# Encoder layer on one core: the residual's gate computed beside the first attention units in four column tiles from 1 MB loads, with the interleaving constants set anew

## The chip, the cores and the metric

The kernel runs on one core of a Trainium2 chip. The metric is device microseconds (us) for one launch. A launch computes one layer for two independent requests of 1024 tokens each, one after the other; below they are called the first and the second group.

## The reference, cut to what matters

Per group, with D = 1024, x of 1024 x 1024 and a condition vector c of 1024:

```
mod = silu(c) @ w_ada + b_ada              # w_ada is 1024 x 3072
shift, scale, gate = split(mod, 3)
h = rms_norm(x) * (1 + scale) + shift
qa, ka, va, za, qb, kb, vb, zb, ga, gb = split(h @ w_in)
oa = gqa_attention(qa, ka, va) * silu(za)                  # 8 heads of 64
ob = headwise_norm(diff_attention(qb, kb, vb)) * silu(zb)  # 4 heads, two maps each
out = (sigmoid(ga) * (oa @ w_proj_a) + sigmoid(gb) * (ob @ w_proj_b)) @ w_out
y = x + gate * out
```

The case is about `gate`: the last third of w_ada (1024 x 1024, 4 MB), multiplied by silu(c) of both groups at once. It is needed only where y is formed, at the very end of a group. It is made once, during the first group, and both groups use it.

## The kernel before, in words

Everything is in f32. Most projections split each f32 operand into a rounded part and a rest (two fp32r tiles) and sum three products; others, among them the gate, are plain f32 matmuls, which the trace records as two passes each, a weight load and a matmul per pass. Wide operands lie in 1 MB buffers ("u", 15 of them); weights come through three 256 KB staging buffers ("st"), are split by ScalarE and GpSimd (L179, L181) and land in two weight buffers ("w"). All DMAs are issued on one queue, SP's.

One group goes through these stages. A head makes k, v and half of the q of branch A. Then the attention runs as a chain of units: phase 0 and phase 1 hold 16 units each of branch A, phases 2 to 5 hold 4 units each of branch B (one phase for each head). A unit's scores (L734, L735) go to PSUM, VectorE takes the maximum (L736), ScalarE the exponential (L738), VectorE transposes blocks (L771), four DMAs finish the transposition ("flip", L776, tile q), and the values' matmuls follow (L796, L797 for A, L836 for B). This chain is long and TensorE would idle beside it, so every phase is woven with projections. Three streams run together: the attention, the projection that the next phase needs (qa_gen, vb_gen, qkb_gen with L514), and "z units" (z_gen, L703: 24 matmuls of 512 columns, an eviction by L709, a store), which nothing needs until the end of the group. There are 48 z units in a group. Six of them go to the head, and Z_SHARE gives a number to each phase; the last phase takes what is left.

The function `weave` (L72) sets the order by hand: each stream has a declared length and a head start, and the stream that is least far along goes next. The constants Z_SHARE, Z_HEAD_A, ATT_W (a factor on the attention's length), IN_A and Z_A (head starts) set the pace of each phase. A scheduler then lays out each engine's instructions in one fixed order from this emission order and its own estimate of time.

The last phase (L1150) weaves the rest of the attention, a stream `gates` (gated_gen, L909: it loads attention outputs and z units back, multiplies them, splits them into u buffers; its last part is kept for later) and a stream `fill`. In the first group `fill` starts with the gate (gate_gen, L445), then the remaining z units, then the first 16 - TAIL of the 16 steps of branch A's merge (merge_gen, L953: 12 matmuls of 512 columns for a step, and a multiplication by VectorE, L987, with the sigmoid of a reloaded z unit). The other TAIL steps follow when the attention is over. During the attention, general PSUM work has three banks; after it (`alone[0] = True`), L121 lets it take two more. Branch B's merge and the output projection (out_gen, L990) end the group; L1010 reads the gate, `gatec`.

gate_gen before: for each half of the 1024 gate channels it takes one PSUM bank, and for each of 8 row chunks loads 256 KB through a staging buffer (L451) and issues one f32 matmul with 2 stationary columns, the two groups' silu(c), and 512 moving columns, all 8 summed in the bank (L452). VectorE copies the 2 x 512 result (L456), four small TensorE transposes turn it into columns (L459), and L461 adds the bias. The stream yields after every second chunk: 8 steps.

Of the kernel before, what the change touches and what calls it, by code (L numbers as in the profile page):

```python
# [12 lines left out]
F32 = mybir.dt.float32  # L13
F32R = mybir.dt.float32r
AF = mybir.ActivationFunctionType
ALU = mybir.AluOpType
AX = mybir.AxisListType
# [3 lines left out]
P = 128  # L21
T = 1024
D = 1024
NCH = D // P
# [10 lines left out]


Z_SHARE = (
    (7, 19, 5, 3, 3, 4),
    (9, 14, 7, 3, 2, 6),
)  # L40
Z_HEAD = (6, 6)
Z_HEAD_A = (-0.4, -0.45)
ATT_W = (
    (1.07, 0.837, 1.1, 0.95, 1.07, 1.52),
    (1.15, 1.354, 1.035, 1.15, 0.85, 1.069),
)
IN_A = (
    (0.1, 0.05, 0.2, 0.05, 0.15, 0.1),
    (0.1, -0.05, 0.45, 0.15, 0.15, 0.65),
)  # L50
Z_A = (
    (0.1, 0.0, 0.4, 0.0, 0.0, 0.0),
    (0.15, 0.05, 0.35, 0.15, -0.1, -0.1),
)
LAST_ATT, LAST_FILL = (44, 26)
GATED_A = -0.3
TAIL = 6
TAIL_A = 0.3
LAG = 2

SILU = 2

# [9 lines left out]
def weave(*streams):  # L72

    live = [[g, n, 0, ahead] for g, n, ahead in streams if n > 0]
    while live:
        s = min(live, key=lambda s: s[2] / s[1] - s[3])
        if next(s[0], None) is not None:
            s[2] += 1
        else:
            live.remove(s)  # L80
# [10 lines left out]
def kernel(ctx: ExitStack, tc: tile.TileContext, t: dict):  # L91
    nc = tc.nc
    ent = ctx.enter_context

    const = ent(tc.tile_pool(name="const", bufs=1))
    upool = ent(tc.tile_pool(name="upool", bufs=15))
    wpool = ent(tc.tile_pool(name="wpool", bufs=2))
    spool = ent(tc.tile_pool(name="spool", bufs=3))
# [12 lines left out]
    def nm(s):  # L111
        uid[0] += 1
        return f"{s}_{uid[0]}"

    def sbank():
        return ps_s.tile([P, 1024], F32, tag="s", name=nm("s"))
# [4 lines left out]
    def gbank():  # L121
        turn[0] += 1
        if alone[0] and turn[0] % 5 in (0, 2):
            return sbank()[:, :512]
        return fbank()

    def fbank():
        return ps_f.tile([P, 512], F32, tag="f", name=nm("f"))

    def utile():  # L130
        return upool.tile([P, 2048], F32R, tag="u", name=nm("u"))

    def chunks4(u):
        return u.rearrange("p (c n) -> p c n", c=4)
# [18 lines left out]
    def mtile(tag, shape, dt=F32, bufs=None):  # L153
        return mpool.tile(shape, dt, tag=tag, name=nm(tag), bufs=bufs)

    def rtile():
        return mtile("row", [P, 512], bufs=3)

    dma = nc.sync.dma_start
# [4 lines left out]
    w_ada = t["w_ada"][0]  # L164
# [3 lines left out]
    ident = const.tile([P, P], F32, name="ident")  # L168
# [2 lines left out]
    nc.vector.memset(ones_c, 1.0)  # L171
    nhalf = const.tile([P, 32], F32, name="nhalf")
    nc.vector.memset(nhalf, -0.5)


    def split_w(w, q, st):
# [11 lines left out]
    def load_w(pieces, early=False):  # L188

        w = wpool.tile([P, NCH, 2, 256], F32R, tag="w", name=nm("w"))  # L190
        sts = []
        for q in range(4):
            if early:
                if q % 2 == 0:
                    room = halves2(ptile())
                st = room[q % 2].rearrange("p (c n) -> p c n", c=2)
            else:
                st = spool.tile([P, 2, 256], F32, tag="st", name=nm("st"))
            sts.append(st)
            off = 0  # L200
            for src in pieces(q):
                n = src.shape[1]
                dma(st[:, :, off : off + n], src.rearrange("(c p) n -> p c n", p=P))
                off += n
            assert off == 256
            if not early:
                split_w(w, q, st)
        return (w, sts) if early else w

    def w_cols(mat, *cols):  # L210
        def pieces(q):
            return [mat[q * 256 : (q + 1) * 256, c : c + n] for c, n in cols]
        return pieces
# [16 lines left out]
    bcol = const.tile([P, 3, NCH], F32, name="bcol")  # L230
    gcol = const.tile([P, NCH], F32, name="gcol")
    cT = const.tile([P, NCH, 2], F32, name="cT")
    modc = const.tile([P, 2, NCH, 2], F32, name="modc")
    gatec = const.tile([P, NCH, 2], F32, name="gatec")
# [208 lines left out]


    def gate_gen():  # L445
        for half in range(2):
            acc = gbank()[:2]
            for k in range(NCH):
                st = spool.tile([P, 512], F32, tag="st", name=nm("st"))
                col = 2 * D + half * 512  # L450
                dma(st, w_ada[k * P : (k + 1) * P, col : col + 512])  # L451
                nc.tensor.matmul(acc, cT[:, k], st, start=(k == 0), stop=(k == NCH - 1))  # L452
                if k % 2:
                    yield 1
            row = rtile()[:2]
            nc.vector.tensor_copy(row, acc)  # L456
            ps = gbank()[:, :8].rearrange("p (c g) -> p c g", g=2)
            for c in range(4):
                nc.tensor.transpose(ps[:, c, :], row[:, c * P : (c + 1) * P], ident[:2, :2])  # L459
            cs = slice(half * 4, half * 4 + 4)  # L460
            nc.vector.tensor_tensor(  # L461
                out=gatec[:, cs], in0=ps, in1=bcol[:, 2, cs].unsqueeze(2).to_broadcast([P, 4, 2]), op=ALU.add
            )


    def ht_gen(g, ht):
# [105 lines left out]
    def pipelined(ht, w, front, back):  # L572
        pend = []
        for tt in range(NTT):
            ps = yield from proj_tt(ht, w, tt)
            pend.append((tt, front(tt, ps)))
            if len(pend) > LAG:
                back(*pend.pop(0))
# [20 lines left out]
    def v2(u):  # L599
        return u.rearrange("p (h n) -> p h n", h=2)  # L600
# [26 lines left out]
    def qa_gen(st, half):  # L627
        w = load_w(w_cols(w_in, (C_QA + half * 256, 256)))
        qs = [v2(utile()), v2(utile())]
        ht = st["ht"]  # L630
        st["qa"][half] = qs
        if half == 0:

            by_q(st["cosA"], st["sinA"], gqa, 16)

        def front(tt, ps):
            x3, s3 = rows(ps, 4, st["rsA"][:, half, tt])
            rope(x3, s3, st["cosA"][:, tt : tt + 1], st["sinA"][:, tt : tt + 1], 16, by_turns(tt))
            return x3

        def back(tt, x3):
            sl = slice(tt * P, (tt + 1) * P)
            pairs_T(x3, qs[0][:, :, sl], qs[1][:, :, sl])
            made[id(qs)] = tt + 1

        yield from pipelined(ht, w, front, back)
# [371 lines left out]
    def head(g, st, zs, late):  # L1018
# [3 lines left out]
        if g == 0:  # L1022

            for i in range(2):
                weave((islice(kva, 6), 6, 0.0), (islice(zs, 3), 3, 0.0))
                if i == 0:
                    late()
            weave((chain(kva, qa), 40, 0.0), (islice(zs, nz - 6), nz - 6, Z_HEAD_A[g]))
        else:
            weave((chain(kva, qa), 52, 0.0), (islice(zs, nz), nz, Z_HEAD_A[g]))  # L1030

# [48 lines left out]
    def until_next(att):  # L1080

        for mark in att:
            if mark is not None:
                return
            yield 1
# [16 lines left out]
    for g in range(2):  # L1102
        st = states[g]
        ht = st["ht"]
        load_tables_A(st)
        zs = chain(*[z_item(st, i) for i in range(12)])
        head(g, st, zs, late)
        alone[0] = False
        if g == 0:
            load_tables_B()  # L1110

        att = attention(units_of(st))

        def phase(k, *fs, more=()):
            n_att = 16 * (6 + PV_LAG) if k < 2 else 4 * (9 + PV_LAG)
            nz = 3 * Z_SHARE[g][k]
            weave(
                (until_next(att), n_att * ATT_W[g][k], 0.0), (chain(*fs), 31 * len(fs), IN_A[g][k]),
                (islice(zs, nz), nz, Z_A[g][k]), *more,
            )  # L1120

        phase(0, qa_gen(st, 1))
        phase(1, vb_gen(ht, st["vb"], 0), qkb_gen(ht, st["qkb"], 0))
        oT, mT = ([], []), ([], [])
        for h in range(4):
            fs = []
            if h < 3:
                fs.append(qkb_gen(ht, st["qkb"], h + 1))
            if h == 1:
                fs.append(vb_gen(ht, st["vb"], 1))  # L1130
            if h < 3:
                phase(2 + h, *fs)

        first = chain(*[gated_gen(st, i, hf, oT[hf]) for i in range(2) for hf in range(2)])
        then = [[gated_gen(st, i, hf, oT[hf]) for hf in range(2)] for i in (2, 3)]

        def gates():
            yield from first
            yield from chain(*then[0])

        def fill():
            if g == 0:
                yield from gate_gen()
            yield from zs
            drain(first)
            yield from islice(merge, 16 - TAIL)

        merge = merge_gen(st, 0, oT, mT)

        weave((until_next(att), LAST_ATT, 0.0), (fill(), LAST_FILL, 0.0), (gates(), 12, GATED_A))  # L1150
        alone[0] = True
        weave((merge, TAIL, 0.0), (then[1][0], 2, TAIL_A))
        weave((merge_gen(st, 1, oT, mT), 8, 0.0), (then[1][1], 4, 1.0))
        if g == 0:
            weave((out_gen(g, mT), 16, 0.0), (ht_gen(1, states[1]["ht"]), 13, -0.1))
        else:
            drain(out_gen(g, mT))
# [54 lines left out]
```

## Time and profile before

| | us |
|---|---|
| median of 3 runs | 1974.42 |
| lowest and highest run | 1972.81, 1974.46 |
| span of the profiled execution, first to last instruction | 1971.9 |
| TensorE matmuls busy (PE) | 1901.8 |
| TensorE weight loads busy (PEld) | 1619.1 |
| VectorE busy (DVE) | 1353.0 |
| ScalarE busy (ACT) | 1012.0 |
| GpSimd busy (POOL) | 680.9 |

The runs' times are for whole launches; the profiled execution shows its span, 1971.9 us, 2.5 us under the median of the runs. In the rows of the profile a name such as `f<-st,cT` means that the tile f (a PSUM bank) is written from st and cT. `x32` is a count of records; two numbers after a bar are busy time in us and the mean duration of one in ns. Matmul records overlap, because the next starts before the one before has drained: the pace is read from starts, not from durations. A number in square brackets on the timeline is the idle time of the engine before that piece, with what ended it.

### The profile page before, as it was taken

The numbers are of one execution on the slowest core, as the hardware profiler recorded it, in microseconds if no ns is written. First come the engines' busy times: TensorE is split into PE (matmuls) and PEld (weight loads), VectorE is DVE, ScalarE is ACT, GpSimd is POOL, SyncE is SP. The second block draws the span as 40 slices with busy tenths as digits, with TensorE's granted clock in tenths as the row PEclk, the third lists the DMA queues.
The fourth block names the chain that finished last, engine by engine and source line by source line (L and its number), as shares of the span: only waits on it lengthen the run. The fifth ranks groups of instructions, "written<-read, shape, count | busy, mean of one in ns | idle before, by whom it ended". The sixth has DMA issues, their size and how long they took to land. (4 is left out here: it accounts for less than half of the span.)

```text
span 1971.9 us, 30870 instructions
## 1 busy us (share of the span) xinstructions
PE 1901.8 (96%) x10466; PEld 1619.1 (82%) x10466; DVE 1353.0 (69%) x2165; ACT 1012.0 (51%) x1920; POOL 680.9 (35%) x958
## 2 busy tenths in 40 slices
PE   8999999999989999999999999999999999998999
PEld 3888888888878985778889788888888889776887
DVE  4658876786888577757465598768878766776641
ACT  4447655565655353464323576556666444447410
POOL 2363511442446251322235344114444426322210
PEclk9899999999999999999999999999999999999999
DMA  9125545556454345865641355555555334478431
GB/s 315 33 89 149 144 139 149 158 156 174 127 144 111 89 117 173 272 234 179 222 151 44 115 144 167 148 149 157 156 152 161 98 102 119 120 222 267 166 102 75
DMA packets 271614, 295.26 MB, mean 150 GB/s; under 512 B 37856, under 2 KB 220256, under 8 KB 271456
## 3 DMA queue, kind: packets, MB, share of 16 engines
q1 hardware_dynamic: 271456, 293.28, 50.1%
q8 instruction: 84, 1.38, 0.3%
q14 instruction: 74, 0.61, 0.1%
HBM read 133.72 MB, written 42.01 MB: 89 GB/s over the span
## 5 line engine op out<-in xcount | busy, mean ns | idle before, releaser
L703 PE MATMUL f<-u,w 128*128 128x512 f32 x2184 | 561.3, 395 | 3.0 <-ACT w L179 1.3
L514 PE MATMUL f<-w,u 128*128 128x256 f32 x3456 | 489.6, 286 | 5.2 <-ACT ev L709 2.7
L514 PEld LDWEIGHTS f<-w,u 128*128 128x128 f32 x3456 | 460.7, 192 | 26.8 <-ACT ev L709 3.7
L703 PEld LDWEIGHTS f<-u,w 128*128 128x128 f32 x2184 | 396.8, 189 | 78.1 <-ACT w L179 1.8
L181 POOL TENSOR_TENSOR w<-st,w 128x512 fp32r<-128x512 f32 x166 | 227.8, 1391 | 463.2 <-ACT w L179 412.9
L736 DVE TENSOR_REDUCE m<-s 128x1 f32<-128x1024 f32 x256 | 310.2, 1217 | 55.1 <-PE s L735 52.0
L771 DVE STREAM_TRANSPOSE p<-p 128x1024 f32<-128x1024 f32 x192 | 238.0, 1241 | 112.8 <-ACT p L738 110.2
L785 DVE TENSOR_TENSOR q<-q,hi 128x512 fp32r<-128x512 f32 x256 | 193.9, 774 | 47.9 <-ACT hi L784 46.4
L738 ACT ACTIVATE p<-s,m,rsB 128x1024 f32<-128x1024 f32 x128 | 154.0, 1204 | 135.0 <-DVE m L737 103.3
L738 ACT ACTIVATE p<-s,m,rsA 128x1024 f32<-128x1024 f32 x128 | 153.8, 1202 | 128.1 <-DMA q<-p 95.8
L735 PE MATMUL s<-u,sw 128*128 128x512 f32 x512 | 205.0, 401 | 0.0
L784 ACT ACTIVATE hi<-q 128x512 fp32r<-128x512 f32 x256 | 153.2, 624 | 78.2 <-DMA q<-p 50.2
L179 ACT ACTIVATE w<-st 128x512 fp32r<-128x512 f32 x196 | 114.2, 626 | 101.9 <-DMA st<-in_w_in_dram 46.6
L976 PE MATMUL f<-u,w 128*128 128x512 f32 x552 | 136.4, 400 | 11.3 <-ACT ev L709 4.1
L796 PE MATMUL a<-hi,u 128*128 128x256 f32 x512 | 132.0, 284 | 4.8 <-DVE oo L813 3.1
L976 PEld LDWEIGHTS f<-u,w 128*128 128x128 f32 x552 | 104.8, 192 | 35.3 <-DVE u L987 4.6
L836 PE MATMUL a<-q,u 128*128 128x256 f32 x512 | 125.9, 385 | 5.6 <-DMA q<-p 1.9
L797 PE MATMUL a<-q,u 128*128 128x256 f32 x512 | 129.8, 287 | 0.5 <-DVE q L785 0.4
L734 PE MATMUL s<-u 128*128 128x512 f32 x256 | 109.5, 428 | 7.9 <-ACT p L738 4.0
L734 PE MATMUL s<-u,u 128*128 128x512 f32 x256 | 103.3, 404 | 13.8 <-ACT p L738 9.0
L836 PEld LDWEIGHTS a<-q,u 128*128 128x128 f32 x512 | 95.9, 193 | 21.6 <-issue 2.9
L735 PEld LDWEIGHTS s<-u,sw 128*128 128x128 f32 x512 | 97.4, 190 | 15.5
(186 smaller groups left out, 2639.1 us busy)
## 6 DMA issues: line engine op xcount, KB each, us to landing
q<-p SPq DMA_DIRECT2D x768, 128.0 KB, 2.6
st<-in_w_in_dram SPq DMA_DIRECT2D x132, 256.0 KB, 3.0
zd<-ev SPq DMA_DIRECT2D x96, 256.0 KB, 2.2
sw<-u SPq DMA_DIRECT2D x256, 64.0 KB, 2.0
p<-zd SPq DMA_DIRECT2D x64, 256.0 KB, 3.8
u<-in_w_ada_dram SPq DMA_DIRECT2D x8, 1024.0 KB, 10.4
st<-in_w_in_dram SPq DMA_DIRECT2D x64, 128.0 KB, 2.7
st<-in_w_out_dram SPq DMA_DIRECT2D x32, 256.0 KB, 3.2
```

What stands on the lines that cost most here:

```text
L181: e.tensor_tensor(out=wl, in0=st, in1=wh.bitcast(F32), op=ALU.subtract)
L514: nc.tensor.matmul(ps, lt[c][:, sl], w[:, c, wi, :], start=(k == 0), stop=(k == 23))
L703: nc.tensor.matmul(ps, w[:, c, wi, e * P : (e + 1) * P], rt[c], start=(k == 0), stop=(k == 23),)
L734: nc.tensor.matmul(s[:, sl], q, k[:, sl], start=True, stop=False)
L735: nc.tensor.matmul(s[:, sl], sw, k[:, sl], start=False, stop=True)
L736: nc.vector.tensor_reduce(out=m, in_=s, axis=AX.X, op=ALU.max, negate=True)
L738: nc.scalar.activation(pt.rearrange("p (j c a) -> p j c a", j=4, c=8), s.rearrange("p (c a j) -> p j c a", c=8, j=4), AF.Exp, scale=rs, bi ...
L771: nc.vector.transpose(pt, pt)
L784: nc.scalar.activation(th, tl.bitcast(F32), AF.Copy)
L785: nc.vector.tensor_tensor(out=tl, in0=tl.bitcast(F32), in1=th.bitcast(F32), op=ALU.subtract)
L836: nc.tensor.matmul(acc, u["v"][:, k], pT[:, k], start=(k == 0), stop=(k == 7))
L976: nc.tensor.matmul(ps, w[:, c, wi, d * P : (d + 1) * P], o[:, oi, :], start=(k == 0), stop=(k == 11))
```

## The change

The gate leaves the last phase and becomes a fourth stream of the first group's phase 0, with declared length 12 and a head start of -0.2. It comes in four pieces n, one for each half of the channels and each half of the rows. A piece is one load of 1 MB into a u buffer; then a PSUM bank is zeroed by VectorE and four f32 matmuls (2 stationary columns, 512 moving columns) write to partitions 0, 32, 64 and 96 of the bank, each with its own column tile of the TensorE array and each started and stopped by itself, so that nothing is summed in the bank; ScalarE copies the bank to SBUF. Four more f32 matmuls with the copied rows as 128 x 128 stationary operand and a constant 128 x 2 matrix `two` as the moving one both transpose and sum the four partial rows. VectorE adds the bias for the first half of the rows, and the earlier result for the second.

The last phase's fill loses the gate, gets one more z unit in the first group (taken from phase 1), and TAIL falls from 6 to 3 in both groups, so three more merge steps are emitted in the last phase. The other constants of the weaving change too, in both groups.

```diff
 Z_SHARE = (
-    (7, 19, 5, 3, 3, 4),
+    (7, 18, 5, 3, 3, 5),
     (9, 14, 7, 3, 2, 6),
 )
-Z_HEAD_A = (-0.4, -0.45)
+Z_HEAD_A = (-0.4, -0.5)
 ATT_W = (
     (1.07, 0.837, 1.1, 0.95, 1.07, 1.52),
-    (1.15, 1.354, 1.035, 1.15, 0.85, 1.069),
+    (1.133, 1.218, 1.035, 1.15, 0.917, 1.069),
 )
 IN_A = (
-    (0.1, 0.05, 0.2, 0.05, 0.15, 0.1),
-    (0.1, -0.05, 0.45, 0.15, 0.15, 0.65),
+    (0.15, 0.05, 0.2, 0.05, 0.25, 0.1),
+    (-0.1, -0.15, 0.45, 0.25, 0.15, 0.85),
 )
 Z_A = (
-    (0.1, 0.0, 0.4, 0.0, 0.0, 0.0),
-    (0.15, 0.05, 0.35, 0.15, -0.1, -0.1),
+    (0.1, 0.0, 0.2, 0.05, 0.0, 0.0),
+    (0.15, 0.05, 0.45, 0.15, -0.1, -0.1),
 )
-LAST_ATT, LAST_FILL = (44, 26)
+LAST_ATT = (45, 44)
+LAST_FILL = (24, 26)
-TAIL = 6
+TAIL = 3
+GATE_A = -0.2
...
+    two = const.tile([P, 2], F32, name="two")
+    nc.vector.tensor_reduce(
+        out=two, in_=ident.rearrange("p (j r) -> p r j", j=4)[:, :2, :], axis=AX.X, op=ALU.add
+    )
...
     def gate_gen():
-        for half in range(2):
-            acc = gbank()[:2]
-            for k in range(NCH):
-                st = spool.tile([P, 512], F32, tag="st", name=nm("st"))
-                col = 2 * D + half * 512
-                dma(st, w_ada[k * P : (k + 1) * P, col : col + 512])
-                nc.tensor.matmul(acc, cT[:, k], st, start=(k == 0), stop=(k == NCH - 1))
-                if k % 2:
-                    yield 1
-            row = rtile()[:2]
-            nc.vector.tensor_copy(row, acc)
+        for n in range(4):
+            half, q = n // 2, n % 2
+            wt = chunks4(utile().bitcast(F32))
+            row, col = q * 512, 2 * D + half * 512
+            dma(wt, w_ada[row : row + 512, col : col + 512].rearrange("(c p) n -> p c n", p=P))
+            yield 1
+            acc = gbank()
+            nc.vector.memset(acc, 0.0)
+            for c in range(4):
+                nc.tensor.matmul(
+                    acc[32 * c : 32 * c + 2], cT[:, q * 4 + c], wt[:, c], start=True, stop=True,
+                    tile_position=(0, 32 * c),
+                )
+            part = rtile()
+            nc.scalar.activation(part, acc, AF.Copy)
+            yield 1
             ps = gbank()[:, :8].rearrange("p (c g) -> p c g", g=2)
             for c in range(4):
-                nc.tensor.transpose(ps[:, c, :], row[:, c * P : (c + 1) * P], ident[:2, :2])
-            cs = slice(half * 4, half * 4 + 4)
-            nc.vector.tensor_tensor(
-                out=gatec[:, cs], in0=ps, in1=bcol[:, 2, cs].unsqueeze(2).to_broadcast([P, 4, 2]), op=ALU.add
-            )
+                nc.tensor.matmul(ps[:, c, :], part[:, c * P : (c + 1) * P], two, start=True, stop=True)
+            g = gatec[:, half * 4 : half * 4 + 4]
+            b = g if q else bcol[:, 2, half * 4 : half * 4 + 4].unsqueeze(2).to_broadcast([P, 4, 2])
+            nc.vector.tensor_tensor(out=g, in0=ps, in1=b, op=ALU.add)
+            yield 1
...
-        phase(0, qa_gen(st, 1))
+        phase(0, qa_gen(st, 1), more=((gate_gen(), 12, GATE_A),) if g == 0 else ())
...
         def fill():
-            if g == 0:
-                yield from gate_gen()
             yield from zs
...
-        weave((until_next(att), LAST_ATT, 0.0), (fill(), LAST_FILL, 0.0), (gates(), 12, GATED_A))
+        weave((until_next(att), LAST_ATT[g], 0.0), (fill(), LAST_FILL[g], 0.0), (gates(), 12, GATED_A))
```

## The prediction, made before the run

> **What bounds the kernel now.** I read the page's first and second part, then stretches of the span, then the timeline where the gate runs.
>
> ```profile
> span 1971.9 us, 30870 instructions
> PE 1901.8 (96%) x10466; PEld 1619.1 (82%) x10466; DVE 1353.0 (69%) x2165; ACT 1012.0 (51%) x1920; POOL 680.9 (35%) x958
> PE   8999999999989999999999999999999999998999
> ```
>
> TensorE (PE) is busy in 1901.8 of 1971.9 us, in every stretch but the first and a few later ones; the next engine, VectorE, stands at 69%. So the time is TensorE's work at its pace, plus 70 us of idle. A change can do three things: alter what TensorE has to issue, remove or add idle, or put work where there was idle. The idle is spread; here are stretches of the first group's last phase, of the same places in the second group (whose last phase has no gate), and of the phases that receive the gate. Columns: stretch, its length, PE busy (records), granted clock, share of the DMA engines, GB/s.
>
> ```profile
> 751.00:790.00 39.00, 35.18 (x125) 1.00 0.68 206
> 821.00:850.00 29.00, 24.89 (x109) 0.94 0.94 305
> ...
> 1711.00:1750.00 39.00, 39.00 (x179) 1.00 0.60 177
> ...
> 1781.00:1810.00 29.00, 22.36 (x97) 0.94 0.84 282
> ...
> 140.00:350.00 210.00, 203.32 (x1198) 0.99 0.53 146
> 350.00:560.00 210.00, 204.41 (x1189) 1.00 0.56 155
> ...
> 1100.00:1310.00 210.00, 202.33 (x1162) 0.99 0.53 146
> 1310.00:1520.00 210.00, 203.22 (x1208) 0.99 0.56 154
> ```
>
> The gate runs at 751 to 790 and there PE idles 39.00 - 35.18 = 3.8 us; at the same place of the second group it idles for nothing. After the attention's last scores it is the other way round: 4.1 us in the first group (821 to 850), 6.6 in the second (1781 to 1810). Phases 0 and 1 idle 6.7 and 5.6 us of 210 each: they have little room for more work.
>
> **The change, part by part.**
>
> *The gate's matmuls.* Old price first, from the lines grouped by shape (busy us, mean ns, idle before) and from PE's timeline.
>
> ```profile
> L452 PE MATMUL f<-st,cT 128*2 128x512 f32 x32 | 15.2, 592 | 1.5 <-DMA st<-in_w_ada_dram 1.5
> L459 PE MATMUL f<-ident,row 2*128 2x2 f32 x8 | 0.8, 202 | 0.8 <-DVE row L456 0.8
> ```
>
> ```profile
> 751.14 2.74 PE L452 MATMUL f<-st,cT 128*2 128x512 f32 x6
> ...
> 754.38 0.50 PE L858 MATMUL f<-ones_c,at 128*128 128x1 f32 x4
> 754.74 0.49 PE L734 MATMUL s<-u 128*128 128x512 f32 x1
> ...
> 767.73 0.40 PE L459 MATMUL f<-ident,row 2*128 2x2 f32 x4 [0.77 <-DVE row L456]
> 768.07 1.02 PE L452 MATMUL f<-st,cT 128*2 128x512 f32 x2
> ```
>
> Sixteen f32 matmuls are 32 passes. Six passes last 2.74 us from first start to last end and one lasts 0.592, so they start (2.74 - 0.592) / 5 = 0.43 us apart: 32 x 0.43 = 13.8 us. Four transposes take 768.07 - 767.73 = 0.34 us, eight 0.7. Removed: 14.5 us.
>
> Added: four groups of four matmuls, each again two passes of 0.43 us, now on four column tiles. No row here has column tiles, so I bound it. If a tile's pass starts only when the pass before has gone through, a group is 8 x 0.43 + the last pass's tail of 0.592 - 0.43 = 0.16, 3.6 us; if all four tiles stream at once, 2 x 0.43 + 0.16 = 1.0 us. I take a value between. The rows show the passes one behind the other in program order, and the two passes of one matmul need the same tile with other weights, so the second must follow the first. Then in a fixed order only the second pass of one tile and the first of the next can run together: 5 slots, 5 x 0.43 + 0.16 = 2.3 us for a group, 9.2 us for four.
>
> The Trainium skill bears on that from both sides. "TensorE: Matmul & The Clock Gate", Part 3, says that matmuls start and end in strict program order, which is what my five slots use, but it also measured three column tiles at 2.38 times the speed of one, for single passes. By that factor alone, 13.8 us would become an estimated 5.8. "TensorEngine Tiling (Array Packing)", Key Properties, speaks against the change: a change of tiling mode drains the engine, and there would be two in each group. With the tail above as the drain, the second would add 4 x 0.16 = 0.6 us. No run of this case yet shows either.
>
> Then 16 f32 matmuls with a full 128 x 128 stationary operand and 2 columns. The nearest row is L858 (one column): four passes from 754.38 to the next start at 754.74, 0.09 us each. It is lowest there because a load was already made; at the start of the kernel eight such passes stand in a row:
>
> ```profile
> 53.69 1.63 PE L273 MATMUL f<-ones_c,q 128*128 128x1 f32 x7
> 55.18 2.91 PE L703 MATMUL s<-u,w 128*128 128x512 f32 x6
> ```
>
> One of the eight records is missing from the trace; 55.18 - 53.69 = 1.49 us over eight is 0.19 each. Thirty-two passes are then 2.9 to 6.1 us; as the new ones come eight in a row, I take 0.155 us, between the two, 5.0 us. Sum of this edit: -14.5 + 9.2 + 5.0 = **-0.3 us**, with ends 4 x 1.0 + 2.9 - 14.5 = -7.6 and 4 x 3.6 + 6.1 - 14.5 = +6.0.
>
> *The waits around the old gate.* The 3.8 us of idle at 751 to 790 go with it: 1.5 is L452 waiting for its loads and 0.8 is L459 for VectorE, by the rows above; the rest fits the bank that the gate holds from its first matmul to L456, leaving two of three. What takes its place as cover is 24 matmuls of the extra z unit and 36 of three merge steps. Their pace:
>
> ```profile
> 789.73 8.45 PE L703 MATMUL f<-u,w 128*128 128x512 f32 x36
> ```
>
> (8.45 - 0.39) / 35 = 0.23 us, so 60 make 13.8 us, about the 14.5 that leave: the attention keeps its cover. I take **-3.8**; the ends are -3.8 and 0, since the second group, without a gate, loses as much a little later.
>
> *TAIL from 6 to 3.* Three merge steps for each group come into the regime of three banks. The early steps do wait there:
>
> ```profile
> 1784.80 5.78 PE L976 MATMUL f<-u,w 128*128 128x512 f32 x24 [2.61 <-DVE u L987]
> ...
> 1799.12 3.03 PE L976 MATMUL f<-u,w 128*128 128x512 f32 x12 [0.99 <-DVE u L987]
> ...
> 1819.59 8.46 PE L976 MATMUL f<-u,w 128*128 128x512 f32 x36
> ```
>
> But steps 11 to 13, the ones that move, are the last row: 36 matmuls, back to back, in f banks already, with the attention over. I take **0**, with 6 x 0.99 = 6 us as the upper end.
>
> *Phase 0 with the gate, phase 1 without one z unit.* Of the 15 u buffers phase 0 holds 14 (8 for the normalised input, 2 for k and v, 4 for q), so the four 1 MB loads go through one buffer, and each waits on SP's queue for the matmuls of the one before; behind it wait the flips (L776), the q swaps (L593) and the next weights (L203). The stream's three steps per piece stand a twelfth of the phase apart, about 210 / 12 = 17 us:
>
> ```profile
> L250 SPq DMA_DIRECT2D u<-in_w_ada_dram x8: 368/485/2545, 1.2 to 20.7; - x8
> ...
> DMA to landing us min/median/max: 5.4/10.4/12.6
> ```
>
> ```profile
> L776 SPq DMA_DIRECT2D q<-p x133: 542/602/1927, 147.9 to 347.9; - x133
> ...
> DMA to landing us min/median/max: 2.5/2.6/4.0
> ```
>
> A load takes 10.4 us to land, under 17, so the gate itself should find its data. What a flip (2.6 us) loses beside it is the third rival below; here 0. In issues SP gains: 16 become 4.
>
> The zeroing of the bank is a new wait: four matmuls stand behind a VectorE instruction, and all of TensorE behind them.
>
> ```profile
> L736 DVE TENSOR_REDUCE m<-s 128x1 f32<-128x1024 f32 x256 | 310.2, 1217 | 55.1 <-PE s L735 52.0
> 200.00:350.00 150.00, 144.58 (x862) 127.22 (x861) 109.39 (x156) 85.01 (x164) 42.30 (x39) 1.00 0.53 147
> ```
>
> It costs nothing when the order gives it time, and 4 x 1.2 = 4.9 us if each stands behind one reduction. The nearest row is L459's, 0.8 for two: I take **+0.8**. The engines' own time is free: VectorE is busy 109 and ScalarE 85 of 150 us there, and four zeroings, four copies and four additions are under 2 us for each piece.
>
> Against that stands cover. The two phases together get 14.2 us of gate and lose one z unit of 24 x 0.23 = 5.5: 8.7 us more independent work beside the same attention, whose waits there are (PE's waits in 130 to 350, then in 350 to 560; total, times, longest):
>
> ```profile
> PE s L734 <- DMA q<-p: 2.2, 2, 1.4
> PE s L734 <- ACT p L738: 1.4, 2, 0.8
> ...
> PE s L734 <- DMA q<-p: 3.9, 2, 3.6
> PE s L734 <- ACT p L738: 0.8, 1, 0.8
> ```
>
> That is 8.3 us. The order is fixed, so new work shortens a wait only where it happens to stand before it: 0 to -8.3, and I take a quarter, **-2.0**.
>
> *The constants.* They move work within a phase and remove none. The second group, where most of them change, idles 7.7 + 6.8 us in its two long stretches against 6.7 + 5.6 in the first group; bringing one to the other is worth 2.2. I take **0**, with 2.2 either way. The constant `two` is made in the first microseconds, before TensorE has any data, and costs nothing.
>
> **Sum:** -0.3 - 3.8 + 0 + 0.8 - 2.0 = -5.3 us, 1971.9 - 5.3 = 1966.6 of span. The median of the runs lies 2.5 us above the profiled span; with that kept, **1969.1 us**, 0.27% below 1974.42. What a measurement of this kernel can tell from no change is about 0.2%, 3.9 us, so faster means below 1970.5.
>
> **The rivals.**
>
> 1. *All four tiles stream at once.* A group is 1.0 us and not 2.3: 5.2 us less, 1963.9. For it: the tiles share no output partitions, and the compiler may order passes so that no tile waits. Against: passes stand in pairs in every f32 row here. The Trainium skill's section on packing, named above, starts tiles about 4 ns apart.
> 2. *Column tiles bring nothing.* A group is 3.6 us: 4 x 1.3 = 5.2 us more, 1974.3, no change. This is the change not doing what it says; no row speaks for tiles yet.
> 3. *Slower: the 1 MB loads hold up the flips.* A flip's packets share the 16 engines with a load that takes 10.4 us, and the scores behind it wait. The longest wait for a flip in these phases is 3.6 us; if each load makes one, 4 x 3.6 = 14.4 us, 1983.5. It decides from (5.3 + 3.9) / 4 = 2.3 us for each load on. For it: those 3.6 us exist with 256 KB weights as the largest neighbours. Against: the DMA engines are at 0.53 there, and cover stands in the weave.
> 4. *Merge steps wait for banks,* 6 us: 1975.1, no change.
>
> **How the numbers follow.** Forecast 0.38 (its own range 1965 to 1973, three quarters of it under 1970.5), rival 1 0.24, rival 2 0.15, rival 3 0.18, rival 4 0.05. Faster: 0.29 + 0.24 = 0.53. Within 0.2%: 0.09 from the forecast, 0.12 from rival 2, 0.04 from rival 4, 0.25. Slower: 0.18 + 0.03 + 0.01 = 0.22. The range reaches down past rival 1 with some of the cover's lower end, to 1960, and up into rival 3's milder half, to 1980.
>
> **What would show it.** Starts of the tiled passes: a group's eight records within 1.0 us (rival 1), 2.2 (forecast) or 3.5 (rival 2). The records on `two` at 0.09 to 0.19 us apart. No idle where the last phase's gate stood, as in the second group. The landing time of L776's flips in phase 0: near 2.6 us (forecast) or well above, with more waits of L734 on q<-p (rival 3). L976's waits on L987 in both groups no larger. The forecast is wrong if phase 0 gains more idle than the last phase loses, or if the new constants move more than 2.2 us.

## The result and the profile after

The changed kernel takes 1974.12 us (median of 20 runs, 1965.49 to 1991.98) against 1974.44 us for the kernel before (20 runs, 1969.18 to 1979.46). The ratio is 1.0000 with a 95% interval of 0.9987 to 1.0014: no change that can be measured. The forecast of 1969.1 us was 5 us too low, though inside its range; the case that came out had been given 0.25. That the time lies inside the range is luck, as the account step by step below shows: two large errors nearly cancelled.

The first lines of the page of the changed kernel:

```profile
span 1972.5 us, 30913 instructions
PE 1895.7 (96%) x10490; PEld 1625.9 (82%) x10490; DVE 1361.4 (69%) x2170; ACT 1017.6 (52%) x1928; POOL 674.0 (34%) x958
```

TensorE is busy for 6.1 us less, and the span is 0.6 us longer, so idle grew by 6.7 us, from 70.1 to 76.8. First, is the new gate as cheap as it should be? Its two lines in the changed kernel (L462 the tiled matmuls, L471 those on `two`), grouped by shape, then pieces of it on PE's timeline:

```profile
L462 PE MATMUL f<-u,cT 128*2 128x512 f32 x32 | 6.0, 702 | 0.2 <-DVE f L460 0.2
L471 PE MATMUL f<-two,row 128*128 128x2 f32 x32 | 4.5, 264 | 0.0
```

```profile
205.23 1.04 PE L462 MATMUL f<-u,cT 128*2 128x512 f32 x8
206.20 0.44 PE L579 MATMUL f<-ident,row 128*128 128x128 f32 x2
...
216.93 0.95 PE L471 MATMUL f<-two,row 128*128 128x2 f32 x8
217.74 0.36 PE L808 MATMUL a<-hi,u 128*128 128x256 f32 x1
...
238.96 1.03 PE L462 MATMUL f<-u,cT 128*2 128x512 f32 x6
239.92 0.50 PE L746 MATMUL s<-u,u 128*128 128x512 f32 x1
...
241.05 1.02 PE L462 MATMUL f<-u,cT 128*2 128x512 f32 x2
242.00 0.74 PE L526 MATMUL f<-w,u 128*128 128x256 f32 x4
...
269.19 1.89 PE L462 MATMUL f<-u,cT 128*2 128x512 f32 x8
271.01 0.58 PE L808 MATMUL a<-hi,u 128*128 128x256 f32 x1
```

Nearly. The eight passes of the first piece take 206.20 - 205.23 = 0.97 us: all four tiles stream at once, as in rival 1. The eight passes on `two` take 0.81 us, 0.10 each. The second piece was laid out in two parts, six passes and two, with scores between them, and each part takes as long as a whole piece (0.96 and 0.95 us). The last pair of lines shows something else: eight passes took 1.82 us at 269.19, because TensorE ran at half its clock there (a granted clock of 0.50 from 265.55 to 272.38). Read from the starts in this way, with half-clock time counted half, the new gate's work is 4.8 + 3.2 = 8.1 us. The old gate's, whose 32 passes were laid out in eight runs, is 15.7 us in the same reading; the prediction's count had 14.5.

Now the stretches that the prediction showed for before, in the changed kernel (same columns), with the first group's stretch of 690 to 751 as well, which stands first for the kernel before:

```profile
690.00:751.00 61.00, 60.76 (x357) 1.00 0.40 110
```

```profile
690.00:751.00 61.00, 58.26 (x350) 1.00 0.42 109
751.00:790.00 39.00, 39.00 (x181) 1.00 0.53 146
790.00:821.00 31.00, 30.53 (x136) 1.00 0.78 226
821.00:850.00 29.00, 21.98 (x91) 0.88 0.93 279
```

The idle at the old gate's place is gone, as forecast (39.00 of 39.00), but 2.7 us stand just before it and 7.0 us after it, where before had 0.2 and 4.1. To compare whole stages, here they are by their own landmarks: first scores, first values of branch B, first output matmul, the second group's first scores and first output matmul. First before, then the changed kernel:

```profile
140.70:561.10 420.40, 408.83 (x2388) 0.99 0.54 151
561.10:932.70 371.60, 359.88 (x1872) 0.99 0.54 164
932.70:1096.00 163.30, 162.83 (x913) 1.00 0.40 135
1096.00:1881.00 785.00, 756.83 (x4227) 0.99 0.53 152
```

```profile
142.70:567.00 424.30, 411.72 (x2408) 0.98 0.59 155
567.00:931.30 364.30, 352.62 (x1878) 0.99 0.56 160
931.30:1100.60 169.30, 166.07 (x920) 0.99 0.40 133
1100.60:1881.50 780.90, 753.28 (x4223) 0.99 0.56 153
```

Phases 0 and 1 grow by 3.9 us, the rest of the first group's attention and its merge shrink by 7.3, the output and the second group's head grow by 6.0, the second group's attention shrinks by 4.1; the start is 2.0 longer. So from its first scores to its first output matmul the first group did become 3.4 us shorter. The start, ahead of the first scores, has the same matmuls in both kernels in almost the same order, and it took between 137.1 and 142.9 us in the profiles of all the kernels below; its 2.0 us, with 3.4 us of added idle in them, need not be the change's.

**Half-clock time.** The granted clock is not a blur. In the trace it is either 1.00 or 0.50, and the halves come in pieces of 3.41 us or multiples. These are the stretches at half clock in the two kernels, up to the last microsecond, cut to the first and the last and the sum (columns as above), first before, then after:

```profile
43.21:46.62 3.41, 3.41 (x18) 0.50 0.48 57
...
1794.25:1797.66 3.41, 3.41 (x11) 0.50 0.63 216
sum 40.97, PE 39.93; mean PE 4.44
```

```profile
43.68:47.10 3.42, 3.42 (x19) 0.50 0.69 71
...
265.55:272.38 6.83, 6.83 (x32) 0.50 0.45 106
...
1777.65:1787.89 10.24, 5.86 (x14) 0.50 0.72 228
sum 58.04, PE 52.26; mean PE 4.02
```

What brings them on is seen best where the changed kernel stalls for 4.9 us (four stretches of 3.41 us, then PE's waits there):

```profile
1217.88:1221.29 3.41, 2.30 (x16) 1.00 0.23 45
1221.29:1224.70 3.41, 0.00 (x0) 1.00 0.79 192
1224.70:1228.11 3.41, 3.02 (x13) 0.50 0.51 132
1228.11:1231.53 3.42, 3.42 (x18) 1.00 0.68 215
```

```profile
PE a L808 <- DVE oo L825: 4.9, 1, 4.9
```

Here an idle window of 3.41 us is followed by one at half clock. I cut both profiles into windows of this length, starting where the trace changes the clock, and took those after the first 60 us. All 16 in which PE was busy for less than 1.5 us were followed by half clock, and so were all 141 such windows in the fourteen profiles below. Of the 10 with 1.6 to 2.1 us, three were. Of those with more that ran at full clock, none was. Two things stay unexplained: three windows that were at half clock themselves, with PE busy for 2.45, 2.78 and 3.41 us, were followed by another at half clock; and in the first 60 us half clock also followed windows that were wholly busy (39.79 to 43.21 and 46.62 to 50.03 in the kernel before). So a stall that leaves less than 1.5 us of a window busy costs itself and then up to 1.7 us for each half-clock window behind it, which is one window in most of these cases and two or three in some. The Trainium skill, "TensorE: Matmul & The Clock Gate", Part 1, describes this gate: two states, a free-running window of about 3.4 us, half rate after an idle window. The trace agrees in the states and the length; here windows that were up to 1.49 us busy already counted as idle.

With that the span can be split in three: idle (span less PE's busy time), the half-clock loss (half of PE's busy time in half-clock stretches), and the rest, TensorE's work as it would be at full clock. All kernels of this study, in us of the profiled execution, with the ratio of the runs to those of before:

| kernel | span | idle | half-clock loss | rest | ratio, 95% interval |
|---|---|---|---|---|---|
| before | 1971.9 | 70.1 | 20.0 | 1881.8 | |
| changed | 1972.5 | 76.8 | 26.1 | 1869.6 | 1.0000 (0.9987 to 1.0014) |
| before_no_gate | 1977.9 | 86.6 | 27.5 | 1863.8 | 1.0052 (1.0036 to 1.0068) |
| after_no_gate | 1976.4 | 85.7 | 27.4 | 1863.3 | 1.0053 (1.0034 to 1.0073) |
| before_tiles_last | 1996.7 | 91.4 | 33.0 | 1872.3 | 1.0153 (1.0132 to 1.0173) |
| after_one_tile | 1972.1 | 72.7 | 18.4 | 1881.0 | 1.0036 (1.0017 to 1.0056) |
| before_tiles_phase0 | 2010.0 | 98.7 | 41.0 | 1870.3 | 1.0157 (1.0137 to 1.0177) |
| after_old_second | 1988.0 | 86.2 | 29.2 | 1872.6 | 1.0068 (1.0050 to 1.0087) |
| after_nudge | 1982.3 | 83.7 | 26.6 | 1872.0 | 1.0037 (1.0021 to 1.0053) |
| before_nudge | 1986.8 | 79.8 | 25.9 | 1881.1 | 1.0068 (1.0051 to 1.0086) |
| before_nudge_down | 1970.9 | 67.7 | 21.6 | 1881.6 | 0.9995 (0.9978 to 1.0012) |
| after_nudge_z | 1987.3 | 84.8 | 27.9 | 1874.6 | 1.0032 (1.0017 to 1.0047) |
| before_no_gate_nudge | 1991.1 | 92.7 | 34.8 | 1863.6 | 1.0097 (1.0070 to 1.0124) |
| after_no_gate_nudge | 1980.2 | 86.6 | 29.0 | 1864.6 | 1.0016 (1.0000 to 1.0031) |

The rest sorts the kernels by their gate: the three with the old gate have 1881.1 to 1881.8, the six with tiles 1869.6 to 1874.6 (mean 1871.9), the four without a gate 1863.3 to 1864.6 (mean 1863.8), and the new gate with one tile in place of four has 1881.0. By that the old gate's work is worth 17.7 us and the new one's 8.1, and the change takes 12.2 us out of TensorE's work between the two profiles. Idle (+6.7) and half-clock time (+6.1) bring it back.

Not all of the 12.2 is the gate's: 4.5 us of it lie in the start, the output and the second group, whose matmuls the change does not touch, and no run shows why. The first group alone, from its first scores to its first output matmul, is sharper: a rest of 762.2 to 762.5 us with the old gate, 754.0 to 756.0 with tiles, 745.8 to 747.3 without a gate and 764.5 with one tile. There the old gate is worth 15.9 us and the new one 8.4, which agrees with their starts (15.7 and 8.1), and the change takes out 7.7. A profile is one execution, and some lie off the median of their kernel (before_tiles_phase0 was 8 us above it, after_nudge_z 9 above, after_one_tile 7 below); the first group's rest stays within 2 us for kernels of one gate all the same.

### The profile page after: what moved, and what is told of

It reads as the page before. It is cut to its first block, busy times and chain, and to the rows that moved or that the text cites. A ratio compares the mean times of both kernels' runs of the same rounds, so it can differ in the third digit from the quotient of the medians.

```text
span 1972.5 us, 30913 instructions
## 1 busy us (share of the span) xinstructions
PE 1895.7 (96%) x10490; PEld 1625.9 (82%) x10490; DVE 1361.4 (69%) x2170; ACT 1017.6 (52%) x1928; POOL 674.0 (34%) x958
## 4 chain that ended last, share of the span: by engine, by line
PE 60%; DVE 12%; DMA 10%; issue 5%; SPq 5%; ACT 4%; POOL 2%; ACTq 0%; POOLq 0%; DVEq 0%
PE f L715 14%; PE f L526 14%; DMA q<-p 5%; PE f L1017 5%; PE f L988 4%; PE a L848 4%; PE s L1017 4%; SPq L788 4%; PE s L746 4%; PE s L747 3%; DVE m L748 3%; DVE q L797 3%; DVE p L783 2%; PE s L988 2%; PE a L808 2%
## 5 line engine op out<-in xcount | busy, mean ns | idle before, releaser
L715 PE MATMUL f<-u,w 128*128 128x512 f32 x2232 | 574.7, 396 | 2.7 <-DVE ssB L872 2.1
L715 PEld LDWEIGHTS f<-u,w 128*128 128x128 f32 x2232 | 408.0, 190 | 80.2 <-DVE ssB L872 2.3
L988 PE MATMUL f<-u,w 128*128 128x512 f32 x588 | 142.0, 394 | 3.6 <-DVE u L960 2.4
L848 PE MATMUL a<-q,u 128*128 128x256 f32 x512 | 131.1, 393 | 7.6 <-DMA q<-p 6.5
L809 PE MATMUL a<-q,u 128*128 128x256 f32 x512 | 131.5, 289 | 1.7 <-DVE q L797 1.6
L988 PEld LDWEIGHTS f<-u,w 128*128 128x128 f32 x588 | 109.6, 188 | 27.9 <-DVE u L960 3.2
L746 PE MATMUL s<-u,u 128*128 128x512 f32 x256 | 104.1, 407 | 12.6 <-ACT p L750 9.9
L581 ACT ACTIVATE u<-f 64x256 fp32r<-64x256 f32 (+1 forms) x196 | 71.0, 364 | 83.0 <-DVE u L582 60.2
```

Source lines behind the costliest of these rows:

```text
L715: nc.tensor.matmul(ps, w[:, c, wi, e * P : (e + 1) * P], rt[c], start=(k == 0), stop=(k == 23),)
L746: nc.tensor.matmul(s[:, sl], q, k[:, sl], start=True, stop=False)
L848: nc.tensor.matmul(acc, u["v"][:, k], pT[:, k], start=(k == 0), stop=(k == 7))
L988: nc.tensor.matmul(ps, w[:, c, wi, d * P : (d + 1) * P], o[:, oi, :], start=(k == 0), stop=(k == 11))
```

## The experiments

Two theories went in. **W**: TensorE's work decides, the gate's price counts wherever it stands. **C**: the old gate was cover for the last phase, so taking it out gives little. After the first four runs a third came up, **O**: the fixed order decides; any edit makes the scheduler lay out other orders, and these differ by more than the edit is worth.

**Without a gate, before.** The stream's steps remain, its work goes:

```diff
     def gate_gen():
-        for half in range(2):
-            acc = gbank()[:2]
...
+        nc.vector.tensor_copy(gatec, bcol[:, 2, :].unsqueeze(2).to_broadcast([P, NCH, 2]))
+        for _ in range(8):
+            yield 1
```

> The kernel before with the gate's matmuls and loads left out (the gate is set to its bias, so part of the computation is missing); the emission order of all else is the same. Theory W (TensorE's work decides): the old gate's 14.5 us of passes and the 3.8 us of idle beside them go, 1974.4 - 18.3 = 1956 us. Theory C (the old gate was cover for the attention's last units, so it cost little where it stood): the idle that it covered opens, 1968 or more.

Measured: 1980.81 us, slower than with the gate. W falls as it was stated. C gave the right side but no reason for a loss. The stages of this kernel:

```profile
138.30:555.50 417.20, 407.11 (x2389) 1.00 0.55 152
555.50:932.50 377.00, 350.72 (x1832) 0.97 0.51 149
932.50:1100.80 168.30, 164.87 (x913) 0.99 0.41 134
1100.80:1887.00 786.20, 757.59 (x4227) 0.99 0.53 152
```

From the first values of B to the first output matmul it takes 377.0 us, where before takes 371.6 with the gate in it: idle is 26.3 instead of 11.7 and the clock 0.97. Its order on TensorE differs from that of before, apart from the gate, from about 40% of the instructions to the end, through the second group too, although the order of emission is the same.

**Without a gate, after**, with the same edit (12 empty steps).

> The changed kernel with the gate's matmuls and loads left out (the gate is set to its bias, so part of the computation is missing). Theory W: the new gate costs its TensorE time, 4 x 0.97 us of tiled passes and 4 x 0.8 us of the transposing matmuls, so 1974.1 - 7 = 1967 us, and the new constants are then what lost the gain: 11 us slower than the kernel before without its gate. Theory C: the new gate costs more than its work in phase 0 (its loads, the zeroing), 1960 or less, and both kernels without a gate stand within 5 us of each other.

Measured: 1980.74 us, also slower. Neither expected time held. One clause of C did: the two kernels without a gate stand within 5 us of each other. That agrees with their rest, 1863.8 and 1863.3; that idle and half-clock loss together come out alike too, 114.1 and 113.1 us from two different orders, no theory here foresaw.

**The new gate at the old place:** before with gate_gen of the changed kernel and the constant `two`; nothing else.

> The kernel before with the new gate code (column tiles, 1 MB loads) at the old place in the last phase, all constants as before. Theory W: 14.5 us of TensorE work become 7.1, 1974.4 - 7.4 = 1967 us. Theory C: the shorter gate leaves the attention uncovered by as much, 1973 to 1976.

Measured: 2001.05 us, far above both expected times. Its rest is 1872.3, 9.5 below that of before, as W has it; idle is 21.3 us more and the half-clock loss 13.0 more. The new stream also has 12 steps where the old one had 8, so the pace of the fill changed with it. The two largest waits show what the new order costs (PE's waits in 690 to 900; total, times, longest):

```profile
PE s L744 <- ACT p L748: 6.3, 2, 5.8
PE f L868 <- ACT at L861: 4.0, 1, 4.0
```

**One tile for four:**

```diff
-                    acc[32 * c : 32 * c + 2], cT[:, q * 4 + c], wt[:, c], start=True, stop=True,
-                    tile_position=(0, 32 * c),
+                    acc[:2], cT[:, q * 4 + c], wt[:, c], start=(c == 0), stop=(c == 3),
```

> The changed kernel with the four matmuls of a piece summed in one column tile (same loads, same order, same instructions). Theory W: each piece takes 8 passes of 0.43 us one behind the other, 3.5 us for 0.97, 4 x 2.5 = 10 us more, 1984 us. Theory C: phase 0 has idle to take part of it, 1976 to 1980.

Measured: 1981.22 us, 7.1 above the changed kernel, between the two expectations (its order differs from that of the changed kernel in phases 0 and 1, and otherwise only in about a dozen records). The piece itself, in this kernel:

```profile
199.11 3.60 PE L462 MATMUL f<-u,cT 128*2 128x512 f32 x8
202.63 0.44 PE L578 MATMUL f<-ident,row 128*128 128x128 f32 x2
```

3.52 us against 0.97: the four tiles are 3.6 times as fast as one. And phases 0 and 1, which hold the gate here, do pay for work:

```profile
137.10:568.20 431.10, 419.57 (x2408) 0.99 0.58 153
```

They are 431.1 us long, 6.8 more than in the changed kernel, with 7.9 more busy.

**The gate in phase 0 with every constant of before:** the new gate_gen as a stream of phase 0, no z unit moved, TAIL 6.

> The kernel before with the gate moved to the first group's phase 0 in its new form, and every constant of before kept (TAIL 6, the same z units for each phase). Theory O (the last phase's length is set by its fixed order and its attention, not by TensorE's work; the retuned constants are what brings the time back): phase 0 and 1 grow by the gate's 7 us, the last phase keeps its length, 1980 us or more. Theory W (work decides): 7 us less than before, 1966 us.

Measured: 2003.73 us, 29 us slower than before. That is O's side by the time, but not by the place: phases 0 and 1 grew by 4.8 us only, the rest of the first group's attention, which O had keep its length, by 14.4 (386.0 against 371.6), and the output and the second group by 16. The changed kernel has the same gate at the same place and is 30 us faster, by its constants, one z unit and TAIL alone. A third of PE's idle is a single kind of wait (PE's waits, the first; the kernel before has 13.0 us of it in 15 waits):

```profile
PE s L745 <- ACT p L749: 33.9, 19, 4.5
```

**The second group's constants of before in the changed kernel:**

```diff
-Z_HEAD_A = (-0.4, -0.5)
+Z_HEAD_A = (-0.4, -0.45)
...
-    (1.133, 1.218, 1.035, 1.15, 0.917, 1.069),
+    (1.15, 1.354, 1.035, 1.15, 0.85, 1.069),
...
-    (-0.1, -0.15, 0.45, 0.25, 0.15, 0.85),
+    (0.1, -0.05, 0.45, 0.15, 0.15, 0.65),
...
-    (0.15, 0.05, 0.45, 0.15, -0.1, -0.1),
+    (0.15, 0.05, 0.35, 0.15, -0.1, -0.1),
```

> The changed kernel with the second group's constants of before (TAIL stays 3); the first group is untouched and no work changes. Theory O: the constants fit one order only, and the second group, which starts from another state here, loses 4 us or more, 1978 us and up. Theory W: no work changes, within 2 us of the changed kernel, 1972 to 1976.

Measured: 1989.33 us, 15 us above the changed kernel, with no work changed. In its profile 11.1 us of that are in the second group's attention (792.0 against 780.9). In the kernel before these same constants stand beside 1974 us. What fits one schedule does not fit the other.

**Nudges.** One head start moved by 0.05, no work changed:

```diff
-GATE_A = -0.2
+GATE_A = -0.15
```

> The changed kernel with the gate's head start at -0.15 instead of -0.2: no work changes, only the first group's order. Theory O: several us slower, 1977 to 1985, with more idle and half-clock time in the first group. Theory W: 1972 to 1976.

Measured: 1983.27 us, 9 us above the changed kernel, on O's side. In its profile the first group's attention has 3.4 us more idle and 3.9 us more half-clock loss.

```diff
 Z_A = (
-    (0.1, 0.0, 0.4, 0.0, 0.0, 0.0),
+    (0.15, 0.0, 0.4, 0.0, 0.0, 0.0),
```

> The kernel before with the head start of phase 0's z units at 0.15 instead of 0.1: no work changes, only the first group's order (the second group's order on TensorE stays as it is). Theory O: several us slower, 1977 to 1985, lost in the first group alone. Theory W: 1972 to 1976.

Measured: 1986.99 us, above what even O had. Its stages, to be held against those of before:

```profile
140.30:552.50 412.20, 400.22 (x2310) 0.98 0.54 149
552.50:944.30 391.80, 373.23 (x1951) 0.98 0.53 161
944.30:1107.60 163.30, 162.83 (x913) 1.00 0.40 135
1107.60:1895.80 788.20, 759.42 (x4226) 0.99 0.53 152
```

Phases 0 and 1 are 8.2 us shorter (78 matmul records moved behind them) and the next stage 20.2 longer, so the first group loses 12.0. The output and the second group's head, with the same order, take 163.3 us again; its attention is 3.2 longer with the same order, which is less than two executions of one kernel differ by (the runs before go from 1969.18 to 1979.46).

The other direction, 0.05 in the place of 0.1:

> The kernel before with the head start of phase 0's z units at 0.05 instead of 0.1: the nudge of before_nudge in the other direction, no work changed. Theory O: the constants of before sit at a good order and either neighbour loses; 1978 to 1990. If only one direction loses, the nudge is a slope and not a scatter: 1970 to 1975.

Measured: 1972.98 us, the same as before. So it is not a sharp peak with a loss on both sides, as I had put it; in this constant one side is flat over this step.

The nudge of before_nudge in the changed kernel and in the two without a gate:

> The changed kernel with the head start of phase 0's z units at 0.15 instead of 0.1, no work changed. Theory O: 1978 to 1990. Against the kernel before with the same nudge (1987) it shows what the new gate is worth at an order that is tuned for neither: theory W's 7 to 11 us would give 1976 to 1980, none of it 1987.

> before_no_gate with the same nudge, 0.15 for 0.1 (the gate's matmuls and loads are left out, so part of the computation is missing). Against before_nudge (1987): if the gate's 14.5 us of work and its waits count in full, 1969 to 1973; if the old gate was only cover, 1985 to 1989.

> after_no_gate with the same nudge (the gate's matmuls and loads are left out, so part of the computation is missing). Against after_nudge_z: 7 us less if the new gate's TensorE work counts in full; the same or more if the order outweighs it.

Measured: 1980.08, 1993.25 and 1978.40 us. Under this nudge the changed kernel is 7 us faster than the one before (1980 against 1987), at the edge of what W gives. But before_no_gate_nudge, which has 17.5 us less work than before_nudge by the rest, is 6 us slower: idle and half-clock loss are 21.8 us more. That is above both of its expected times. The two changed kernels differ by 1.7 us where 8 to 10 of work lie between them. Neither a full price of work nor a plain cover gives these four numbers. What is left is the order, and its share is as large as that of any of the edits.

## Why the prediction was right and wrong, step by step

- *Column tiles, taken at 2.3 us for a piece: wrong, 0.97.* I reasoned that the two passes of one matmul block the ones behind. All eight weight loads of the piece stand at its start in the trace (x8 in 0.11 us from 205.23), and the four tiles stream through both passes together. Rival 1 had it right. The Trainium skill, "TensorE: Matmul & The Clock Gate", Part 3, on packing, starts tiles almost together; the trace agrees in that. The drain that I priced at 4 x 0.16 us as a possible addition is not seen: 0.97 us is no more than two passes of 0.43 and one tail. The passes on `two`, taken at 0.155, were 0.10: the upper end of 0.19 was read at 53.69 in the kernel before, in a stretch at half clock (50.03 to 60.27), and eight passes on `two` at half clock took 1.63 us here, 0.20 each. By the starts this edit took 7.6 us out (15.7 to 8.1) where the forecast had 0.3.

```profile
205.23 0.11 PEld L462 LDWEIGHTS f<-u,cT 128*2 128x2 f32 x8 [0.35 <-DVE p L783]
```

- *The waits around the old gate, -3.8: gone from their place, not from the stage.* From the first values of B to the first output matmul the idle is 11.7 us in both kernels. The end of 0 that I had named, since "the second group, without a gate, loses as much a little later", was the right one. Of the 1.5 us that I gave to the bank, 0.9 is a wait of L836 for which the profile names no releaser, so the bank was not shown.
- *TAIL, 0:* the waits do not speak against it. For its bank (on L999) L988 waits 0.3 us in the changed kernel, so rival 4 fell. All waits of the merge's matmuls, 2.4 us of them for an operand that L960 had not finished, come to 5.1 us, where before had 11.2. TAIL was not tried alone.
- *The zeroing, +0.8:* 0.2 us by the row of L462 above (2.9 in before_tiles_phase0, so this too is a matter of the order). *Cover, -2.0:* wrong in sign. Phases 0 and 1 idle 11.6 us before and 12.6 after.
- *The 1 MB loads, rival 3:* a load lands in 7.3 us in the median, and the flips beside it are hardly later, except for single ones of up to 7.7 (before: 4.0). Scores waited for a flip 0.6 us in all in this stretch, so the rival fell. The flips (L788) and the loads (L457) of the changed kernel:

```profile
L788 SPq DMA_DIRECT2D q<-p x131: 542/602/2185, 150.9 to 349.4; - x131
...
DMA to landing us min/median/max: 2.6/2.7/7.7
```

```profile
L457 SPq DMA_DIRECT2D u<-in_w_ada_dram x4: 390/456/717, 193.2 to 242.1; - x4
...
DMA to landing us min/median/max: 5.4/7.3/10.2
```

- *The constants, 0 with 2.2 either way: the step that failed most.* I sized them by the idle of the two groups, as if an order could be better or worse by no more than those differ. A step of 0.05 in one head start moved the time by 9 and by 13 us, and four tuples set back moved it by 15. The forecast added small terms on a term that can be larger than all of them. No run has the new constants beside the old gate, so their share and that of the gate's new place are not told apart.
- *The half-clock time was no term at all.* It is 6.1 of the 12.8 us that came back. I had read the clock column as near 1.00 and passed over it, and priced every stall at its own length.

In the forecast's own terms, TensorE's work was to change by -0.3 us, idle by -5.0 and half-clock time by nothing; the two profiles have -12.2, +6.7 and +6.1. Work came out 11.9 us better and the other two 17.8 worse, which leaves the span 5.9 us above its forecast. That the range held is therefore luck: the mechanism was off on both sides. By the first of the signs that I had named the forecast is wrong as well, since phases 0 and 1 gained 1.0 us of idle and the stretch from the first values of B to the output lost none.

So the step on whose account the sum missed is the last but one, the constants: 8 to 12 us of work went, and idle and half-clock time took as much (3.4 us of the idle in the start, where it may be chance). That it is the new order that made them is the best reading of the runs without changed work, and is not shown by a run of its own. What stays open is how much the new gate would gain if both kernels stood at equally well fitted orders. The best of each family that was run are 1974.12 us with tiles and 1972.98 and 1974.44 with the old gate, alike within their intervals. Settling it would take many orders of each. No version that beats both kernels came up, and none was sought beyond these.

## What to carry to other kernels

In a kernel whose order is fixed at build time, do not price an edit by its work alone: find out first what an edit without work costs (move one pacing constant a little, both ways), and take that as the width of every forecast. Split the span into idle, half-clock loss and the rest, and take the rest of the stages that hold the edit: here it showed 7.7 us of work gone where the time showed nothing. And price a stall on TensorE that leaves less than 1.5 us of a 3.41 us window busy at its length and up to 1.7 us more for each half-clock window behind it.

## What the runs showed of the hardware that I had not expected

Four f32 matmuls with 2 stationary columns on four column tiles take 0.97 us where one tile takes 3.52. The clock falls to half even after windows that were 1.47 and 1.49 us busy of 3.41. The clock also goes with the spread between runs of one program: over the 20 runs of the changed kernel the mean granted clock goes from 0.980 (1991.98 us) to 0.990 (1965.49 us), with a correlation of -0.80 and a slope of 1.9 us for each 0.001, which is about 0.1% of the span. Since a stall brings half clock after it, this does not part the one from the other; and it is not so in every kernel (-0.23 over the 12 runs of before_nudge_down).
